# Gathering the last 8 rows of one tile in sixteen by a transfer of their own

## The chip, the cores and the metric

The kernel runs on one core of a Trainium2 chip. The metric is the device time of one execution in microseconds (us); the time quoted for a version is the median of its runs. A profile shows one execution, taken apart by engine: PE (matrix multiplications), DVE and ACT (elementwise work), POOL (here it issues the gathers), SP (here it issues loads and stores), and the 16 DMA engines that move the data.

## What is computed

```python
def setup_inputs():
    B, S, N, D = (16, 4096, 2048, 512)
    return {'x': np.random.randn(B, S, D).astype(np.float32), 'indices': np.sort(np.stack([np.random.choice(S, N, replace=False) for _ in range(B)]), axis=1).astype(np.int64), 'w': np.random.randn(D, D).astype(np.float32)}

def reference(x, indices, w):
    ...
    gathered = x[b_idx, indices, :].copy()
    cs = np.cumsum(gathered, axis=1)
    return np.matmul(cs, w).astype(np.float32)
```

From each of 16 batches 2048 of 4096 rows (512 fp32 numbers, 2 KB each) are picked by a sorted list of indices, summed cumulatively along the list, and multiplied by one 512x512 matrix. 67 MB are read and 67 MB are written.

## The kernel before

The list is cut into tiles of 128 rows (P): 16 tiles in a batch (NT), 256 in all (T). Two tiles make a group (R = 2, G = 128 groups). A tile goes through six steps, each on its own engine, and every engine has its own list of steps with waits on semaphores between them:

1. gather (`gather`, lines 129 to 145, POOL): one indirect DMA at line 139 brings 128 rows, one to a partition, into a slot of `g32`. There are 16 slots (NG), so tile t may be gathered once tile t-16 has been cast; that is the wait on `s_c` in line 132, taken for a whole group. Each slot has its own completion semaphore `s_g[t % 16]`. The row numbers of the first 4 tiles come from a small table `idx_first`, those of all others from `idxg`, which is prepared at the start.
2. cast (`cast`, line 154, ACT): fp32 to fp16, `g32` to `g16`, in the middle of the run two tiles at once. It waits for the gather.
3. sums (`sums`, line 166, PE): four 128x128x128 matmuls with a triangular matrix into PSUM `pa` give the running sums within the tile, transposed.
4. carry (`carry`, lines 185 and 198, DVE): adds the last column of the tile before and writes `cst` in fp16. Line 185 is the copy for the first tile of a batch, where nothing is carried in.
5. project (`project`, line 210, PE): four matmuls with the 512x512 weights into `pb`.
6. drain (`drain`, line 222, ACT) and store (line 245, SP): `pb` to `ob` in fp32, then one store of 1 MB for each two groups.

The order on each engine is written out by hand. ACT does, for u = 0 to 255, the casts listed in `casts[u]` (up to 6 tiles ahead of u) and then the drain of tile u (`step`, lines 393 to 401). PE runs the sums of a tile up to LEAD = 3 tiles or so ahead of the projections. POOL issues the 256 gathers one after the other (lines 308 and 309) and has little else to do after the start. DVE, PE and ACT run the middle of the work in a loop over 16 tiles; POOL and SP have all steps written out. Buffers: 16 slots of `g32`, 16 tiles of `g16`, 4 of `pa`, 8 of `cst`, 4 of `pb`, 16 tiles of `ob`.

At the start SP and ACT load the small index tables (line 251), SP the full index list (line 259), and both the weights, two quarters each (line 264); ACT casts quarters 0 and 1 (line 392), DVE quarters 2 and 3 (line 337), and PE waits for all four before the first projection.

Of the kernel before, what the change touches and what calls it, by code (L numbers as in the profile page):

```python
# [7 lines left out]
P = 128  # L8
FP32 = mybir.dt.float32
FP16 = mybir.dt.float16  # L10
U32 = mybir.dt.uint32
# [22 lines left out]
def kernel(  # L34
# [7 lines left out]
    nc = tc.nc  # L42

    B, S, D = x.shape
    N = indices.shape[1]
    R = 2
    Q = P // R
    DC = D // P
    NT = N // P
    T = B * NT  # L50
    G = T // R
    GB = NT // R
    KI = T // P
    FIRST = 2 * R
    NG = 16
    LEAD = 3
# [2 lines left out]
    NA = 4  # L59
    NB = 4  # L60
    NC = 4
    W = 2
    H = 1
    NO = 4
    U = NT
    V = max(U, W * R * NO)
    assert V % U == 0 and V % (W * R * NO) == 0 and T % V == 0 and U % NG == 0 and U % NA == 0 and U % (R * NC) == 0 and U % NB == 0
    assert D == 512 and N % (R * P) == 0 and T % P == 0

    x_flat = x.rearrange("b s d -> (b s) d")  # L70

    const = ctx.enter_context(tc.tile_pool(name="const", bufs=1))
    ps = ctx.enter_context(tc.tile_pool(name="ps", bufs=1, space=bass.MemoryType.PSUM))

    idx_first = const.tile([P, FIRST, 2], U32)
    idx64 = const.tile([P, KI, 2 * P], U32)
    idxf = const.tile([P, KI, P], FP32)
    idxg = const.tile([P, KI, P], U32)
    w32 = const.tile([P, DC, D], FP32)
# [6 lines left out]
    g32 = [const.tile([P, R, D], FP32, name=f"g32_{i}") for i in range(NG // R)]  # L86
# [8 lines left out]
    def sem(name):  # L95
        return tc.alloc_semaphore(name)
# [4 lines left out]
    s_first = [sem(f"s_first{k}") for k in range(2)]  # L101
    s_w = [sem(f"s_w{c}") for c in range(DC)]
    s_idx = [sem(f"s_idx{k}") for k in range(KI)]
    s_ol = sem("s_ol")
    s_g = [sem(f"s_g{i}") for i in range(NG)]
    s_o = [sem(f"s_o{i}") for i in range(NO)]
# [5 lines left out]
    pool, pe, dve, act, sp = (  # L112
        Lane(e) for e in (nc.gpsimd, nc.tensor, nc.vector, nc.scalar, nc.sync)
    )
# [14 lines left out]
    def gather(t):  # L129
        g, r = divmod(t, R)  # L130
        if t >= NG:
            pool.need(s_c, cast_by[R * (g + 1) - NG - 1])
        if t < FIRST:
            pool.need(s_first[g], 16)
            ap = idx_first[:, t, 0:1]
        else:
            pool.need(s_prep, t // P + 1)
            ap = idxg[:, t // P, t % P : t % P + 1]
        nc.gpsimd.indirect_dma_start(  # L139
            out=g32[g % (NG // R)][:, r, :],  # L140
            out_offset=None,
            in_=x_flat,
            in_offset=bass.IndirectOffsetOnAxis(ap=ap, axis=0),
            element_offset=(t // NT) * S * D,
        ).then_inc(s_g[t % NG], 16)

    PLAIN = (0, 1, G - 2, G - 1)
# [1 line left out]
    def cast(t, n, first=None):  # L150
        g, r = divmod(t, R)
        for u in range(t, t + n):
            act.need(s_g[u % NG], 16 * (u // NG + 1), first)
        nc.scalar.copy(  # L154
            out=g16[g % NH][:, r : r + n], in_=g32[g % (NG // R)][:, r : r + n]
        ).then_inc(s_c, 1)
# [91 lines left out]
    with nc.allow_non_contiguous_dma(reason="a few indices, one per partition"):  # L248
        for k, eng in enumerate((nc.sync, nc.scalar)):
            t = k * R  # L250
            eng.dma_start(
                out=idx_first[:, t : t + R, :],
                in_=indices[0, t * P : (t + R) * P]
                .bitcast(U32)
                .rearrange("(t p w) -> p t w", p=P, w=2),
            ).then_inc(s_first[k], 16)
    idx_rows = indices.bitcast(U32).rearrange("b (t q) -> (b t) q", q=2 * P)
    for k in range(KI):
        nc.sync.dma_start(
            out=idx64[:, k, :], in_=idx_rows[k * P : (k + 1) * P, :]  # L260
# [10 lines left out]
    for i in range(G // W - NO, G // W - 1):  # L271
# [8 lines left out]
        out=ident[:],  # L280
        in_=ident[:],
# [7 lines left out]
        out=ut[:],  # L289
        in_=ut[:],  # L290
# [9 lines left out]
        out=uq[:],  # L300
        in_=uq[:],
# [6 lines left out]
    for t in range(T):  # L308
        gather(t)
# [10 lines left out]
    nc.vector.memset(zeros[:], 0.0).then_inc(s_z, 1)  # L320
    for k in range(KI):
        dve.need(s_idx[k], 16)
        nc.vector.tensor_copy(out=idxf[:, k, :], in_=idx64[:, k, 0::2]).then_inc(s_if, 1)  # L323
    busy(9)
    for k in range(KI):
# [3 lines left out]
            out=pb[k % NB][:, :P], in_=idxf[:, k, :], identity=ident[:]  # L329
# [21 lines left out]
    done = 0  # L351
    for u in range(T):
        lead = 1 if min(u, T - 1 - u) < R * R else min(LEAD, 2 + (u + 4) // 16, 2 + (T - 1 - u) // 15)
        first = u if u // R in PLAIN else u // R * R + R - 1
# [38 lines left out]
    def step(u, first=None):  # L393
        if first is None and u == min(W * R * NO, 2 * U - 1):
            act.need(s_of, 16 * (R + W - 1 - H))
        if u % (W * R) == 0:
            stored = first if first is None else first * (16 * H) // (R * W * NO)
            act.need(s_o[u // R // W % NO], 16 * H * (u // R // W // NO), stored)
        for t, n in casts[u if first is None else 2 * U + u]:
            cast(t if first is None else t - 2 * U, n, first)  # L400
        drain(u, first)
# [40 lines left out]
```

## Time and profile before

| what | us |
|---|---|
| median of 3 runs (lowest, highest) | 438.41 (437.76, 445.43) |
| the profiled execution | 440.94 |
| its span, from the first to the last instruction | 439.2 |
| PE matmul busy | 329.8 |
| ACT busy | 263.6 |
| POOL busy | 243.7 |
| DVE busy | 178.4 |

How to read it: busy times are sums over instructions of one engine, so that an engine with less than 439.2 us has waited for the rest. The mean granted clock of PE was 0.892 of full speed. The page also gives the mean busy share of the 16 DMA engines in 40 slices of the span, and for each queue the packets that they moved; it doesn't tell the 16 engines apart. A row of an instruction group ends with the idle time of the engine just before these instructions and the releaser of most of it.

### The profile page before, as it was taken

The numbers are of one execution on the slowest core, as the hardware profiler recorded it, in microseconds if no ns is written. First come the engines' busy times: TensorE is split into PE (matmuls) and PEld (weight loads), VectorE is DVE, ScalarE is ACT, GpSimd is POOL, SyncE is SP. The second block draws the span as 40 slices with busy tenths as digits, with TensorE's granted clock in tenths as the row PEclk, the third lists the DMA queues.
The fourth block names the chain that finished last, engine by engine and source line by source line (L and its number), as shares of the span: only waits on it lengthen the run. The fifth ranks groups of instructions, "written<-read, shape, count | busy, mean of one in ns | idle before, by whom it ended". The sixth has DMA issues, their size and how long they took to land.

```text
span 439.2 us, 6408 instructions
## 1 busy us (share of the span) xinstructions
PE 329.8 (75%) x2066; PEld 171.5 (39%) x2066; DVE 178.4 (41%) x263; ACT 263.6 (60%) x407; POOL 243.7 (55%) x266
## 2 busy tenths in 40 slices
PE   6518687777877786679787697768777697876995
PEld 2203343343434343335344353434334343443552
DVE  2104343444344444345344344344345353543552
ACT  4216566556665665576656575566576666665794
POOL 6764557565655566556565465565555665655300
PEclk9756989798989899988899698996989969998898
DMA  7864979799888999989898899988989999999966
GB/s 225 256 212 156 347 273 344 252 336 364 285 318 304 333 351 328 350 294 339 316 353 295 310 336 335 359 318 273 366 310 328 331 337 328 300 330 349 331 242 241
DMA packets 39884, 135.68 MB, mean 309 GB/s; under 512 B 5825, under 2 KB 6081, under 8 KB 39873
## 3 DMA queue, kind: packets, MB, share of 16 engines
q0 software_dynamic: 20480, 67.13, 47.9%
q1 hardware_dynamic: 18832, 67.90, 38.9%
q10 hardware_dynamic: 560, 0.53, 0.4%
q8 instruction: 5, 0.08, 0.1%
q14 instruction: 7, 0.05, 0.0%
HBM read 68.42 MB, written 67.11 MB: 309 GB/s over the span
## 4 chain that ended last, share of the span: by engine, by line
PE 74%; issue 10%; DVE 7%; another core or an unknown queue 7%; ACT 1%; DVEq 0%; ACTq 0%; SPq 0%
PE pb L210 55%; PE pa L166 18%; DVE cst L198 7%; PE pb L316 1%; DVE cst L185 0%; ACT ob L222 0%; ACT g L154 0%; PE pb L328 0%; DVEq L26 0%; DVE zeros L320 0%; DVEq L437 0%; ACTq L26 0%; SPq L93 0%
## 5 line engine op out<-in xcount | busy, mean ns | idle before, releaser
L210 PE MATMUL pb<-w,cst 128*128 128x512 f16 x1024 | 293.1, 414 | 84.7 <-DVE cst L198 60.1
L139 POOL DMA_INDIRECT g<-in_x_dram,idxg x252 | 238.2, 945 | 165.1 <-ACT g L154 97.6
L198 DVE TENSOR_TENSOR cst<-pa,cst 128x512 f16<-128x512 f32 x240 | 166.1, 692 | 231.3 <-PE pa L166 162.2
L222 ACT COPY ob<-pb 128x512 f32<-128x512 f32 x256 | 146.2, 591 | 164.6 <-PE pb L210 108.1
L210 PEld LDWEIGHTS pb<-w,cst 128*128 128x128 f16 x1024 | 94.3, 104 | 164.9 <-DVE cst L198 65.8
L154 ACT CAST g<-g 128x1024 f16<-128x1024 f32 (+1 forms) x147 | 138.4, 945 | 0.3 <-issue 0.2
L166 PE MATMUL pa<-ut,g 128*128 128x128 f16 x992 | 103.9, 230 | 16.0 <-issue 12.8
L166 PEld LDWEIGHTS pa<-ut,g 128*128 128x128 f16 x992 | 81.5, 104 | 87.7 <-issue 33.8
L185 DVE CAST cst<-pa 128x512 f16<-128x512 f32 x16 | 11.0, 686 | 16.2 <-PE pa L166 12.6
L316 PE MATMUL pb<-zeros 128*128 128x512 f16 x16 | 5.9, 538 | 1.5 <-DVE zeros L320 1.5
L139 POOL DMA_INDIRECT g<-in_x_dram,idx_first x4 | 4.0, 994 | 1.6 <-issue 0.9
L166 PE MATMUL pa<-uq,g 128*128 128x128 f16 x32 | 3.1, 219 | 1.9 <-issue 1.8
L166 PEld LDWEIGHTS pa<-uq,g 128*128 128x128 f16 x32 | 2.2, 97 | 4.2 <-issue 3.1
L316 PEld LDWEIGHTS pb<-zeros 128*128 128x128 f16 x16 | 2.1, 135 | 4.2 <-issue 2.2
L392 ACT CAST w<-w 128x512 f16<-128x512 f32 x2 | 1.1, 616 | 3.4 <-DMA w<-in_w_dram 3.4
L389 ACT ACT_TABLE_LOAD x1 | 1.3, 1283 | 2.5 <-issue 2.5
L323 DVE CAST idxf<-idx 128x128 f32<-128x128 uint32 x2 | 0.5, 227 | 3.8 <-DMA idx<-in_indices_dram 3.8
L337 DVE CAST w<-w 128x512 f16<-128x512 f32 x2 | 0.8, 422 | 1.6 <-DMA w<-in_w_dram 1.6
L328 PE MATMUL pb<-ident,idxf 128*128 128x128 f32 x2 | 0.9, 447 | 0.0
L328 PEld LDWEIGHTS pb<-ident,idxf 128*128 128x128 f32 x2 | 0.4, 206 | 0.9 <-issue 0.9
L320 DVE MEMSET zeros<- 128x256 uint32 x1 | 0.3, 272 | 1.1 <-SPq L93 1.1
L334 DVE CAST idxg<-pb 128x128 uint32<-128x128 f32 x2 | 0.6, 292 | 0.3 <-PE pb L328 0.2
(11 smaller groups left out, 2.1 us busy)
## 6 DMA issues: line engine op xcount, KB each, us to landing
out_dram<-ob SPq DMA_DIRECT2D x62, 1024.0 KB
g<-in_x_dram,idxg POOLq DMA_INDIRECT x252
out_dram<-ob SPq DMA_DIRECT2D x4, 256.0 KB, 2.8
out_dram<-ob SPq DMA_DIRECT2D x2, 512.0 KB, 3.4
w<-in_w_dram ACTq DMA_DIRECT2D x2, 256.0 KB, 3.3
w<-in_w_dram SPq DMA_DIRECT2D x2, 256.0 KB
idx<-in_indices_dram SPq DMA_DIRECT2D x2, 128.0 KB, 2.6
g<-in_x_dram,idx_first POOLq DMA_INDIRECT x4
```

Of the source, the lines that this page charges most:

```text
L139: nc.gpsimd.indirect_dma_start(out=g32[g % (NG // R)][:, r, :], out_offset=None, in_=x_flat, in_offset=bass.IndirectOffsetOnAxis(ap=ap, ax ...
L154: nc.scalar.copy(out=g16[g % NH][:, r : r + n], in_=g32[g % (NG // R)][:, r : r + n]).then_inc(s_c, 1)
L166: mm = nc.tensor.matmul(out=pa[t % NA][:, c], lhsT=g16[g % NH][:, r, c * P : (c + 1) * P], rhs=uq[:] if first is None and g in PLAIN else ...
L185: nc.vector.tensor_copy(out=dst, in_=src).then_inc(s_d, 1)
L198: nc.vector.tensor_tensor(out=dst, in0=src, in1=last, op=mybir.AluOpType.add).then_inc(s_d, 1)
L210: mm = nc.tensor.matmul(out=pb[u % NB][:], lhsT=cst[g % NC][:, c, j, :], rhs=w16[:, c, :], start=(c == 0), stop=(c == DC - 1),)
L222: nc.scalar.copy(out=ob[g // W % NO][:, g % W, j], in_=pb[u % NB][:]).then_inc(s_e, 1)
L316: nc.tensor.matmul(out=pb[NB - 1][:], lhsT=zeros[:, :P], rhs=zeros[:], start=True, stop=True)
L328: nc.tensor.transpose(out=pb[k % NB][:, :P], in_=idxf[:, k, :], identity=ident[:]).then_inc(s_pt, 1)
L337: nc.vector.tensor_copy(out=w16[:, c, :], in_=w32[:, c, :]).then_inc(s_wc, 1)
L389: nc.scalar.copy(out=spare[:], in_=zeros[:, :1])
L392: nc.scalar.copy(out=w16[:, c, :], in_=w32[:, c, :]).then_inc(s_wc, 1)
```

## The change

In each batch the ninth tile (t % 16 == 8, SPLIT = NT // 2) is gathered by two transfers instead of one. First comes an instruction that puts the cursor of the software-generated transfers back to its start, then a transfer of the last 8 rows (E = 8) with row numbers from a new table `idx_last`, then one of the first 120 rows. The 8 rows report to a semaphore of their own, `s_h`, and the 120 rows to `s_g` as before. The cast of such a tile waits for both. `idx_last` (8 partitions, 16 batches) is loaded once at the start, by a DMA on ACT's queue between the small index table and the weights, and POOL waits for it once (`s_last`). The other 15 tiles of a batch are gathered as before. That makes 16 resets and 272 gathers in place of 256. Nothing on PE, DVE or SP changes, and on ACT only the waits and the one load.

```diff
+    E = 8
+    SPLIT = NT // 2
...
+    idx_last = const.tile([E, B, 2], U32)
...
-        nc.gpsimd.indirect_dma_start(
-            out=g32[g % (NG // R)][:, r, :],
-            out_offset=None,
-            in_=x_flat,
-            in_offset=bass.IndirectOffsetOnAxis(ap=ap, axis=0),
-            element_offset=(t // NT) * S * D,
-        ).then_inc(s_g[t % NG], 16)
+        parts = [(0, P, ap, s_g[t % NG])]
+        if t % NT == SPLIT:
+
+            pool.need(s_last, 16)
+            nc.gpsimd.inc_swdge_sem([], [], mode="reset_dge_cursor")
+            parts = [
+                (P - E, P, idx_last[:, t // NT, 0:1], s_h),
+                (0, P - E, ap[: P - E], s_g[t % NG]),
+            ]
+        for a, b, ap, done in parts:
+            nc.gpsimd.indirect_dma_start(
+                out=g32[g % (NG // R)][a:b, r, :],
+                out_offset=None,
+                in_=x_flat,
+                in_offset=bass.IndirectOffsetOnAxis(ap=ap, axis=0),
+                element_offset=(t // NT) * S * D,
+            ).then_inc(done, 16)
...
             act.need(s_g[u % NG], 16 * (u // NG + 1), first)
+            if u % NT == SPLIT:
+                act.need(s_h, 16 * (u // NT + 1), first)
...
+        nc.scalar.dma_start(
+            out=idx_last[:],
+            in_=indices[:, (SPLIT + 1) * P - E : (SPLIT + 1) * P]
+            .bitcast(U32)
+            .rearrange("b (p w) -> b p w", w=2)
...
+        ).then_inc(s_last, 16)
```

More of the change, by code (lines that the diff above doesn't have):

```diff
@@ L66 @@
     V = max(U, W * R * NO)
-    assert V % U == 0 and V % (W * R * NO) == 0 and T % V == 0 and U % NG == 0 and U % NA == 0 and U % (R * NC) == 0 and U % NB == 0
+    assert U == NT == NG and V % U == 0 and V % (W * R * NO) == 0 and T % V == 0 and U % NG == 0 and U % NA == 0 and U % (R * NC) == 0 and U % NB == 0
     assert D == 512 and N % (R * P) == 0 and T % P == 0
@@ L103 @@
     s_idx = [sem(f"s_idx{k}") for k in range(KI)]
+    s_last = sem("s_last")
+    s_h = sem("s_h")
     s_ol = sem("s_ol")
@@ L256 @@
             ).then_inc(s_first[k], 16)
+        nc.scalar.dma_start(
+            out=idx_last[:],
+            in_=indices[:, (SPLIT + 1) * P - E : (SPLIT + 1) * P]
+            .bitcast(U32)
+            .rearrange("b (p w) -> p b w", w=2),
+        ).then_inc(s_last, 16)
     idx_rows = indices.bitcast(U32).rearrange("b (t q) -> (b t) q", q=2 * P)
```

## The prediction

> **What bounds the kernel now.** I read the page first, then the waits, then busy time by stretch, then the timeline of one stretch in the middle. From the list of instruction groups:
>
> ```profile
> L210 PE MATMUL pb<-w,cst 128*128 128x512 f16 x1024 | 293.1, 414 | 84.7 <-DVE cst L198 60.1
> L139 POOL DMA_INDIRECT g<-in_x_dram,idxg x252 | 238.2, 945 | 165.1 <-ACT g L154 97.6
> L222 ACT COPY ob<-pb 128x512 f32<-128x512 f32 x256 | 146.2, 591 | 164.6 <-PE pb L210 108.1
> L154 ACT CAST g<-g 128x1024 f16<-128x1024 f32 (+1 forms) x147 | 138.4, 945 | 0.3 <-issue 0.2
> ```
>
> The last row decides. The cast is the only reader of gathered rows, and in 147 casts ACT was idle 0.3 us before one: in this execution no cast waited for a gather. The second row says the reverse: it is POOL that waits, 97.6 us, for casts to free slots. So gathers run as far ahead as 16 slots allow. Counting along POOL's and ACT's lists, the gather of tile 116 is issued at 188.19 us and its cast begins at 212.41, 24 us later.
>
> The list of waits, longest first in total (us, times, longest):
>
> ```profile
> DVE cst L198 <- PE pa L166: 162.2, 118, 5.7
> ACT ob L222 <- PE pb L210: 108.1, 81, 3.5
> POOL g L139 <- ACT g L154: 97.6, 42, 5.1
> ```
>
> DVE and ACT wait for PE. PE's full pace shows in the starts of its projections, 205.81, 206.90, 207.98: 1.087 us a tile, 256 tiles x 1.087 = 278 us, and at the granted clock of 0.892 312 us. The span is 439.2, so 127 us are neither. The timeline says what some of that is (start, us, engine, and in brackets the idle time before and its releaser):
>
> ```profile
> 206.67 0.39 PE L166 MATMUL pa<-ut,g 128*128 128x128 f16 x4
> ...
> 209.48 0.95 POOL L139 DMA_INDIRECT g<-in_x_dram,idxg  x1 [0.30 <-issue]
> ...
> 211.87 0.69 DVE L185 CAST cst<-pa 128x512 f16<-128x512 f32 x1 [4.29 <-PE pa L166]
> ...
> 213.41 1.04 PE L210 MATMUL pb<-w,cst 128*128 128x512 f16 x4 [2.71 <-DVE cst L198]
> 213.72 0.94 POOL L139 DMA_INDIRECT g<-in_x_dram,idxg  x1 [3.29 <-ACT g L154]
> ```
>
> The sums at 206.67 are those of tile 112; their reader, the carry at L185, starts 4.8 us after the matmuls are recorded as done (207.06). PE's word comes late; then DVE, ACT, PE and POOL stand still in turn. By stretch (busy us and number for PE, PEld, DVE, ACT, POOL; PE clock; DMA share; GB/s):
>
> ```profile
> 204.00:208.00 4.00, 4.00 (x33) 2.28 (x31) 1.91 (x3) 3.16 (x5) 3.02 (x4) 1.00 1.04 362
> 208.00:212.00 4.00, 2.49 (x19) 1.16 (x16) 0.13 (x1) 0.66 (x2) 1.89 (x2) 1.00 0.98 363
> 212.00:216.00 4.00, 2.59 (x12) 1.18 (x13) 3.33 (x5) 3.86 (x6) 1.89 (x2) 0.83 0.69 214
> ```
>
> The DMA engines are full while PE's word is late (0.98) and slack when work resumes (0.69). So the DMA engines are no idle bystander: between 50 and 400 us their share is 0.87 to 0.94. Why PE is late I can't tell; that it goes with full DMA engines I see. The change touches them in two ways.
>
> **What the Trainium skill says.** "DMA: Bandwidth & Descriptors", section "Why a DMA increments its semaphore by 16 and not by 1": a transfer runs on the largest number up to 16 that divides its slowest dimension; with fewer than 16, the software path takes consecutive engines from a round-robin cursor, and all 16 report completion whatever the shape. So 8 rows go to 8 engines and 120 rows to 15. If the reset sets the cursor to 0 (the page has no reset), these are 0 to 7, then 8 to 15 and 0 to 6, and engine 7 is left out. Same page, "Latency and other measured facts": engines 7 and 15 are usually slower, cause uncertain. That is the gain to be had; this page of the profile doesn't separate the engines, so no row agrees or disagrees. What agrees is the packet count: 20480 on the gather queue is 80 a gather, 16 completions and 64 of two rows.
>
> **The change, part by part.**
>
> Engine loads. In 16 tiles an engine gathers 16 x 8 = 128 rows; after, engine 7 has 121, engines 0 to 6 129, engines 8 to 15 128. Gathers are 67.13 of 135.68 MB, so engine 7 loses 7/128 x 0.495 = 2.7% of its bytes and seven engines gain 0.4%. If engine 7 sets the pace throughout, that is 0.027 x 439.2 = 11.9 us; if nobody waits for it, 0. As no cast waits for a gather, I take 0. Stores (no row shows a wait for one in mid-run: "DMA out" releases 2.2 us, at the end) don't raise it.
>
> POOL. 16 more gathers. A 128-row gather takes 0.945 us and 0.30 of issue; the 8-row one costs between the issue alone and the full 1.25. I take 1.25, as the part that rows cost is unknown. The 120-row one I take as unchanged, up to 1.25 more if its shape is slow. The reset isn't in this trace: between 0 and the 0.30 of a step, taken at 0.1. Per batch 1.35 us (0.3 to 2.8), 16 x 1.35 = 22 us of POOL. The cover is POOL's 97.6 us of waiting for casts, 6.1 a batch, and behind it the 24 us between issue and cast: the split tile and those behind it land some 1.35 us later and still wait. Cost 0. Were the cover gone, it would be the full 22 us. POOL has nothing else queued behind these but gathers; SP's stores aren't passed by it.
>
> ACT. One more wait in 16 casts, on a semaphore raised long before: below the 0.3 us that all 147 casts wait now. Queued behind is the drain of the same step, which holds `pb`, which holds PE; as the wait is met, 0.
>
> Completions and packets. Per batch 16 more completions and 8 one-row packets in place of 4 two-row ones: 20 more packets in 1280, some 320 in all, of completion or half size. Below 0.5% of DMA work, or 2 us if the DMA engines set the end; taken at 0.
>
> Start. The new load stands ahead of ACT's two weight loads and delays them by one issue, 0.49 us (the first index load on that queue). They land 3.3 us after issue at 1.5 and 2.1, near 5.4, then 5.9; ACT's cast of the weights starts at 7.44, when quarter 0 from SP's queue, issued at 2.49, has come. Cover 1.5 us; cost 0, and 0.5 if it is gone. POOL's wait for the table falls before the ninth gather, at 13.40, long after. Nothing more is stored or multiplied.
>
> Sum against the profiled execution: 439.2 + 0 in the span, 440.94 + 0 in all, which stands 2.5 above the median of 438.41. On the median: 438.41 + 0, rounded to 438.5.
>
> **Rivals.**
>
> Relief: engine 7 is the straggler that the full DMA stretches wait for, and PE's word comes when it is done. For it: DMA share near 1 while PE is late. Against it: no cast waits for a gather, and engine 15 stays as it was. Time: at most 438.4 - 11.9 = 426.5; likelier half, as the next engine takes over, 432.5.
>
> Longer bursts, the slower side: POOL issues in bursts (203.24 to 210.43, then a wait to 213.72), and PE's late word ends near the end of such a burst. If late signals last as long as gathers are being written, each batch's extra 1.35 us stretches one burst and the standstill with it: 16 x 1.35 = 22 us, 460; half of it, if only bursts near the limit count, 449. It decides from some 0.55 us a batch (8.8 us, 2%). For it: the coincidence above. Against it: the cause may run the other way, as standing ACT ends POOL's burst.
>
> The change doesn't do what it says: the reset doesn't place the cursor at 0, or 120 rows go to fewer engines. At another cursor the relief falls on another engine: 438.5 again. With 8 engines for 120 rows each gets 15 in place of 8 once in 16 tiles, 7/128 more rows on each such engine, 2.7% more bytes: up to 450.
>
> **How the numbers follow.** Hidden altogether: 0.66, range 434 to 443 (packets and start above, a little relief below). Relief: 0.15, half of it over 2%. Longer bursts: 0.14, nearly all over 2%. Misplaced: 0.05, half each way. A time below 429.6 is faster by over 2%, one above 447.2 slower, which is about what a measurement of this kernel can tell from no change (three runs lie between 437.76 and 445.43). Faster: half of the relief and a little, 0.09. Slower: 0.13 of bursts, 0.02 misplaced, 0.01, together 0.16. Same: 0.75. The range takes in half the relief and the half price of the bursts: 431 to 449.
>
> **What would show it.** Right: the 120- and 8-row gathers appear as 32 rows of POOL near 0.95 us or less; POOL's wait for casts falls from 97.6 by about 22; the cast's idle time stays below 1 us; 20800 packets on the gather queue; DVE's wait for PE stays near 162. Relief would show as DVE's and ACT's waits for PE falling by some 10 us. Longer bursts would show as those waits growing. Wrong altogether: the cast waiting for gathers, or a reset that takes microseconds.

## The result, and the profile after

| | median, us (lowest to highest, runs) |
|---|---|
| before | 440.81 (437.76 to 445.43, 4) |
| after | 465.93 (461.47 to 467.15, 4) |
| ratio, with its 95% interval | 1.058 [1.045, 1.070] |

The change costs 25 us, 5.8%. The forecast was 438.5, within 431 to 449. The profiled execution took 465.24 us with a span of 463.3, 24.1 more than the span of 439.2 before. Ratios are taken over comparable runs only, so they can differ a little from the quotient of the medians given. Every comparison is with runs of the kernel before on the same chip, which matters here: that kernel takes 436 to 448 us on the chips of the first runs and 349 to 352 us on those of the last ones, for a reason that no run shows.

The groups of instructions of the kernel after, to be set beside the four rows shown of before:

```profile
L227 PE MATMUL pb<-w,cst 128*128 128x512 f16 x1024 | 297.4, 418 | 103.4 <-DVE cst L215 86.3
L154 POOL DMA_INDIRECT g<-in_x_dram,idxg x252 | 240.5, 954 | 140.1 <-ACT g L171 70.7
...
L171 ACT CAST g<-g 128x1024 f16<-128x1024 f32 (+1 forms) x147 | 138.3, 944 | 0.3 <-issue 0.2
...
L154 POOL DMA_INDIRECT g<-in_x_dram,idx_last x16 | 14.4, 900 | 32.5 <-ACT g L171 27.9
```

Casts still wait for nothing (0.3 us), so the gathers are not late. A gather of 8 rows takes POOL 0.900 us, nearly as long as one of 128 (0.945 before). PE's projections now wait 86.3 us for DVE in place of 60.1. PE's matmuls themselves take 335.3 us in place of 329.8 (the granted clock is 0.877 in place of 0.892), so slower matmuls are at most 5.5 us of the 24; the rest is waiting.

The longest waits of the kernel after (us in total, times, longest):

```profile
DVE cst L215 <- PE pa L183: 172.1, 115, 4.3
POOL g L154 <- ACT g L171: 98.6, 43, 5.0
...
ACT ob L239 <- PE pb L227: 91.8, 73, 4.8
PE pb L227 <- DVE cst L215: 86.3, 38, 7.6
POOL g L154 <- issue: 75.0, 228, 1.9
```

DVE's wait for PE grew by 9.9 us. A further wait of DVE, whose releaser the profile can't place (it writes `remote`), grew by 23.1 us; first before, then after:

```profile
DVE cst L198 <- remote: 44.7, 16, 12.6
```

```profile
DVE cst L215 <- remote: 67.8, 21, 11.2
```

POOL does 16.7 us more (260.4 busy in place of 243.7), and its idle time before gathers has not shrunk to make room: 98.6 us for casts (97.6 before) and 75.0 between issues (68.4 before). Busy time and these two waits come to 409.7 before and 434.0 after. The difference, 24.3, is the growth of the span (24.1) to within 0.2. It isn't lost at the start or the end: the stretch from 50 to 250 us, first before and then after (busy us and number for PE, PEld, DVE, ACT, POOL; PE clock; DMA share; GB/s):

```profile
50.00:250.00 200.00, 151.67 (x963) 79.25 (x962) 84.36 (x123) 122.62 (x186) 116.25 (x123) 0.91 0.90 319
```

```profile
50.00:250.00 200.00, 147.44 (x917) 77.10 (x918) 79.41 (x116) 117.21 (x179) 117.49 (x124) 0.88 0.85 302
```

POOL issues as many gathers in 200 us as before (124 against 123), but of these some 7 are now of 8 rows. Data moves at 302 GB/s in place of 319, and PE, DVE and ACT get through some 4 to 6% fewer instructions in the stretch. POOL's timeline around one split tile of the kernel after:

```profile
204.64 0.90 POOL L154 DMA_INDIRECT g<-in_x_dram,idx_last  x1 [1.60 <-ACT g L171]
205.84 1.00 POOL L154 DMA_INDIRECT g<-in_x_dram,idxg  x1 [0.30 <-issue]
207.15 0.99 POOL L154 DMA_INDIRECT g<-in_x_dram,idxg  x1 [0.31 <-issue]
208.44 0.96 POOL L154 DMA_INDIRECT g<-in_x_dram,idxg  x1 [0.31 <-issue]
...
216.44 0.95 POOL L154 DMA_INDIRECT g<-in_x_dram,idxg  x1 [3.28 <-ACT g L171]
```

0.90 and 0.30 for the transfer of 8 rows, and 0.05 + 0.04 + 0.01 for neighbours that take a little longer than 0.95: about 1.3 us more, as forecast. The reset is no row of its own and leaves no gap. The wait of 3.28 us that ends the burst stands as it did before (3.29).

### The profile page after: what moved, and what is told of

Its sections match the earlier page's. It is cut to its first block, busy times and chain, and to the rows that moved or that the text cites. A ratio compares the mean times of both kernels' runs of the same rounds, so it can differ in the third digit from the quotient of the medians.

```text
span 463.3 us, 6444 instructions
## 1 busy us (share of the span) xinstructions
PE 335.3 (72%) x2066; PEld 174.1 (38%) x2066; DVE 178.7 (39%) x263; ACT 264.1 (57%) x407; POOL 260.4 (56%) x282
## 4 chain that ended last, share of the span: by engine, by line
PE 68%; another core or an unknown queue 13%; DVE 9%; issue 6%; DMA 1%; SPq 0%; ACT 0%; DVEq 0%
PE pb L227 51%; PE pa L183 18%; DVE cst L215 9%; DMA w<-in_w_dram 1%; ACT ob L239 0%; DVE w L360 0%; SPq L282 0%; DVE cst L202 0%; DVEq L26 0%; ACT g L171 0%; SPq L268 0%; SPq L287 0%; SPq L460 0%; SPq L96 0%
## 5 line engine op out<-in xcount | busy, mean ns | idle before, releaser
L227 PE MATMUL pb<-w,cst 128*128 128x512 f16 x1024 | 297.4, 418 | 103.4 <-DVE cst L215 86.3
L227 PEld LDWEIGHTS pb<-w,cst 128*128 128x128 f16 x1024 | 95.6, 106 | 187.0 <-DVE cst L215 93.4
L183 PE MATMUL pa<-ut,g 128*128 128x128 f16 x992 | 105.7, 233 | 14.6 <-issue 14.3
L183 PEld LDWEIGHTS pa<-ut,g 128*128 128x128 f16 x992 | 82.5, 105 | 86.0 <-issue 33.7
L154 POOL DMA_INDIRECT g<-in_x_dram,idx_last x16 | 14.4, 900 | 32.5 <-ACT g L171 27.9
```

Source lines behind the costliest of these rows:

```text
L154: nc.gpsimd.indirect_dma_start(out=g32[g % (NG // R)][a:b, r, :], out_offset=None, in_=x_flat, in_offset=bass.IndirectOffsetOnAxis(ap=ap, ...
L183: mm = nc.tensor.matmul(out=pa[t % NA][:, c], lhsT=g16[g % NH][:, r, c * P : (c + 1) * P], rhs=uq[:] if first is None and g in PLAIN else ...
L227: mm = nc.tensor.matmul(out=pb[u % NB][:], lhsT=cst[g % NC][:, c, j, :], rhs=w16[:, c, :], start=(c == 0), stop=(c == DC - 1),)
```

## The experiments

Accounts of the missing 24 us that had to be told apart, with their numbers in the texts put on record before each run: POOL's extra time (theory 1); the reset (2), or which DMA engines the two parts fall on and in what shapes (3); the wait that the cast has for a second semaphore; more work for the DMA engines; or the added gather itself, as a transfer that POOL's software makes, while it is under way (4).

### What part of the change it is (first kind of chip)

Kernel before, with the reset alone:

```diff
+        if t % NT == NT // 2:
+            nc.gpsimd.inc_swdge_sem([], [], mode="reset_dge_cursor")
```

> The kernel before, with the cursor reset ahead of the ninth gather of each batch and nothing else: no split, no new table. Theory 1 (any extra time of POOL in a burst of gathers is added to the end): the reset is short, so within 3 us of the 440.8 of before. Theory 2 (the reset itself disturbs the queue of gathers, by some 1.5 us each time): 16 x 1.5 = 24 us more, near 465. Theory 3 (the uneven shapes of 8 and 120 rows on the DMA engines cost the time): no change.

446.7 us (437.62 to 452.37, 20 runs) beside 444.9; ratio 0.991 [0.984, 0.999], which rests on only two of the 20. The medians differ by 1.8 us, in a spread of 15. By neither number is the reset more than a small part of the 25 us.

Kernel after, without the reset:

```diff
-            nc.gpsimd.inc_swdge_sem([], [], mode="reset_dge_cursor")
```

> The changed kernel without the reset: the 8 and the 120 rows go to whichever engines come next. Theory 1: near 464, since POOL still issues 16 more gathers. Theory 2: back near 441. Theory 3: near 464, too, as the shapes stay; if it matters which engine is left out, some us away from 465.9.

467.35 us (466.86 to 474.78, 4); 1.046 [1.039, 1.054]. The change had 1.058 [1.045, 1.070]; the intervals overlap, and most of the cost, if not all, stays. So it doesn't hang on where the cursor stands.

Kernel after, without the reset and cut into 64 and 64 rows:

```diff
-    E = 8
+    E = 64
...
-            nc.gpsimd.inc_swdge_sem([], [], mode="reset_dge_cursor")
```

> The split at 64 and 64 rows, without the reset: as many gathers on POOL as in the changed kernel, but both transfers divide evenly over the 16 DMA engines, 4 rows each. The new table at the start is 64 instead of 8 rows deep, 1024 small packets in place of 128, for which I allow 1 us. Theory 1: near 465. Theory 2: near 441. Theory 3: near 441.

471.69 us (469.07 to 476.76, 4); 1.060 [1.051, 1.069]. In its profile the first drain starts at 18.88 us where it is 12.08 in the run without reset, so some 7 us of it are lost once, at the start; the rest is the cost of the split again. Two even parts are no cheaper than an uneven pair: neither 8 rows nor 120 is a bad shape.

### POOL's time, DMA work, or a gather (first kind of chip)

Each of these three is the kernel before, with one thing added per batch. First, POOL busy with a memset of some 0.96 us:

```diff
+        if t % NT == NT // 2:
+            pool.need(s_idle, t // NT)
+            nc.gpsimd.memset(idle[:], 0.0).then_inc(s_idle, 1)
```

> The kernel before, with one memset of 128x1024 fp32 on POOL ahead of the ninth gather of each batch: some 1 to 1.5 us of POOL's time and no DMA work. The resets alone cost nothing, the split at 8 and 120 rows without reset and the split at 64 and 64 cost as much as the change, so the cost comes with the second gather. Theory 1 (POOL's own time is on the path): 16 x 1 to 1.5 us more than before, 457 to 469. Theory 4 (it is the second gather as a piece of DMA work, with its own descriptors and completions, not POOL's time): within 4 us of before, near 441 to 448.

445.52 us (440.51 to 452.35, 20) beside 442.65; 1.0045 [1.001, 1.008], 2 us. Second, a gather of 8 rows into a spare buffer that nobody reads:

```diff
+        if t % NT == NT // 2:
+            pool.need(s_x, 16 * (t // NT))
+            nc.gpsimd.indirect_dma_start(
+                out=extra[:8],
...
+                in_offset=bass.IndirectOffsetOnAxis(ap=ap[:8], axis=0),
...
+            ).then_inc(s_x, 16)
```

> The kernel before, with a gather of 8 rows into a spare tile ahead of the ninth gather of each batch. Nothing waits for it but its own successor a batch later; the ninth gather keeps its 128 rows, and no table is loaded. Theories 1 and 4: as the change, 463 to 470, since POOL issues as many gathers. If instead the later arrival of the split tile, or the wait on two semaphores, costs the time: within 4 us of before.

468.1 us (466.4 to 469.1, 4); 1.060 [1.051, 1.069]: 26.6 us, 1.66 for each of the 16. Two runs that give POOL almost the same time side by side; POOL's groups and its waits, first with the memset,

```profile
L143 POOL MEMSET idle<- 128x1024 f32 x16 | 15.3, 955 | 28.1 <-ACT g L159 27.0
```

```profile
POOL g L144 <- ACT g L159: 55.9, 27, 4.3
POOL idle L143 <- ACT g L159: 27.0, 10, 3.8
```

and then with the gather of 8 rows:

```profile
L143 POOL DMA_INDIRECT extra<-in_x_dram,idxg x16 | 14.1, 884 | 23.8 <-ACT g L165 20.8
```

```profile
POOL g L150 <- ACT g L165: 79.3, 38, 3.9
...
POOL extra L143 <- ACT g L165: 20.8, 6, 7.3
```

With the memset POOL's waits for casts fall from 97.6 to 55.9 + 27.0 = 82.9, by 14.7, which is what the 15.3 us of memsets took: cover, as the prediction had it. With the gather they are 79.3 + 20.8 = 100.1. POOL had 14.1 us more to do, and waited no less. (The 97.6 are of the profile before, of an earlier run; the next run below, on the chip of these two, has 103.8.) So on these chips POOL's time is covered and a gather is not, though no one waits for its data. The second semaphore of the cast isn't needed for the cost either. The price of 1.66 us is close to the kernel's own pace: before, POOL issued 123 gathers in 200 us, one each 1.63 us. A gather of 8 rows, then, adds about as much time as one of 128 rows takes up on average; no run on this kind of chip added one of 128.

Third, DMA work without POOL: one more load of 128 rows (256 KB) on SP's queue in each batch, 4.2 MB in all, 3% of the traffic.

```diff
+        if g % GB == 2 * W:
+            sp.need(s_x, 16 * b)
+            nc.sync.dma_start(out=extra[:], in_=x_flat[b * S : b * S + P, :]).then_inc(s_x, 16)
```

> The kernel before, with one more load of 128 rows of 2 KB per batch from SP's queue into a spare tile that nobody reads: 4 MB of DMA work more (3%), 16 more completions a batch, nothing on POOL. Theory 1: within 4 us of before. If DMA work of any kind is on the path: 256 KB take some 0.65 us at the 400 GB/s of full stretches, so 16 x 0.65 = 10 us more, near 455.

442.5 us (438.61 to 446.45, 20) beside 442.65; 1.002 [0.998, 1.005]. Sixteen times the rows of the added gathers, moved from SP's queue in 144 packets each where a gather of 8 rows makes 32, cost nothing that shows. It is not the load on the DMA engines, in bytes or in packets.

Last, no gather at all: SP loads every second row of each tile's half in its place, as many bytes, in the order in which the steps need them. POOL is left with 1.5 us of work.

```diff
-        nc.gpsimd.indirect_dma_start(
+        nc.sync.dma_start(
+            out=g32[g % (NG // R)][:, r, :], in_=x_even[b, h * P : (h + 1) * P, 0, :]
         ).then_inc(s_g[t % NG], 16)
```

> The gathers are left out: each tile is loaded by an ordinary DMA from SP's queue, 128 rows of 2 KB, every second row of x, in place of the rows that the indices name; as many bytes to the same slots, and POOL has nothing to do after the start. Theory 1: well below before, since POOL's 20 us of issue a batch are gone: PE's 312 us plus start and end, 340 to 400. If the DMA work is the bound and not who issues it: near 440.

349.7 us (349.67 to 349.84, 4); 0.792 [0.785, 0.798]. Its waits, and its stretch from 100 to 300 us (columns as above):

```profile
DVE cst L190 <- PE pa L158: 145.6, 237, 1.9
ACT g L146 <- DMA out_dram<-ob: 69.8, 53, 2.2
```

```profile
100.00:300.00 200.00, 170.65 (x1210) 89.70 (x1209) 104.43 (x152) 148.51 (x228) 0.00 (x0) 1.00 1.03 403
```

The DMA engines are full throughout (1.03), moving 403 GB/s, and yet DVE never waits longer than 1.9 us for PE, where before it was 5.7. So full DMA engines alone are not what delays PE's word. PE's granted clock is 0.99 in these four runs, where the kernel before has 0.89 to 0.93 on the same chip: the lower clock isn't fixed by the chip. In this run the gathers are gone, and with them the standstills, 93 us worth.

### The same on the other kind of chip

The runs that follow fell on chips where the kernel before takes 350 us. Both kernels once more, unchanged:

> The kernel before, for its profile on the same chip. Where it takes 350 us, casts should wait for gathers and stores (DMA), POOL hardly for casts, and the DMA engines should be busy to 0.95 or more; where it takes 440 us, the profile should look like the first one: casts wait for nothing, POOL for casts.

350.04 us (348.85 to 351.34, 16) beside 350.01; 1.000 [0.999, 1.001].

> The changed kernel as it is, on whichever chip comes. Where before takes some 440 us: 465 again. Where before takes some 350 us: if the DMA engines are the bound there and the left-out engine is the slowest one, up to 2.7% less, 341 to 348; if an added gather costs what it cost in the runs with 64 of them (75/64 = 1.2 us), 16 x 1.2 = 19 us more, 369; if only its DMA work counts, 350 to 352.

362.99 us (362.63 to 363.26, 5); 1.037 [1.035, 1.038]: 13.0 us, half of what it costs on the other chips. Waits of the kernel before there, then of the kernel after:

```profile
DVE cst L198 <- PE pa L166: 139.2, 236, 1.9
...
POOL g L139 <- issue: 71.0, 233, 0.3
ACT g L154 <- DMA g<-in_x_dram,idxg: 69.8, 92, 1.9
...
POOL g L139 <- ACT g L154: 6.7, 22, 0.3
```

```profile
ACT g L171 <- DMA g<-in_x_dram,idxg: 86.8, 75, 4.1
...
POOL g L154 <- ACT g L171: 4.0, 13, 0.3
```

By its profile it is another kernel. POOL hardly waits for casts (6.7 us): it issues one gather after the other, and the casts wait for gathers (69.8, then 86.8). POOL has no waiting left that could cover anything. The gathers' own view gives the sum. First and last start are in it, before and then after, and the page gives the spans of 347.1 and 361.3:

```profile
L139 POOL DMA_INDIRECT g<-in_x_dram,idxg x252: 942/946/955, 8.4 to 322.1; - x126
...
DMA to landing us min/median/max: 3.6/9.0/13.8
```

```profile
L154 POOL DMA_INDIRECT g<-in_x_dram,idxg x252: 942/946/1124, 8.4 to 343.2; - x126
```

The last gather starts 21.1 us later, 16 x 1.32, which is the forecast's price of a batch (1.35). From there to the end it was 25.0 us and is 18.1. So 21.1 - 6.9 = 14.2 us remain in the span. Before, gathers land 9.0 us after issue, up to 13.8; after, the median is 6.6 and the longest 8.7. The DMA engines were behind POOL, and 7 us of this backlog are all the cover there is.

If that is so, the memset must cost as well here. The kernel with the memset again:

> The kernel before with one memset of 0.955 us on POOL ahead of the ninth gather of each batch, no DMA work. Where before takes 350 us and POOL's time is the path: 16 x 0.95 to 1.25 us less what POOL can still hide (some 6 us): 359 to 366. If the change's cost there is DMA work: 350 to 352. Where before takes 440 us: no change, as measured.

356.09 us (355.71 to 356.52, 4) beside 349.86; 1.018 [1.014, 1.022]. In its gathers' view (span 354.0),

```profile
L144 POOL DMA_INDIRECT g<-in_x_dram,idxg x252: 942/946/998, 8.4 to 335.5; - x126
...
DMA to landing us min/median/max: 3.5/6.8/8.5
```

the last gather starts 13.4 us later than before, and the tail is 18.5 us, the backlog gone (8.5 at most): 13.4 - 6.5 = 6.9, and 6.2 measured. POOL's time alone explains the loss on these chips; on the others the memset cost 2 us.

Three sizes of the added transfer, one to a batch or one to four tiles; what was expected of them reckons with the 442 us of the first kind of chip, on which they did not fall. A gather of all 128 rows that nobody reads:

```diff
-                out=extra[:8],
+                out=extra[:],
...
-                in_offset=bass.IndirectOffsetOnAxis(ap=ap[:8], axis=0),
+                in_offset=bass.IndirectOffsetOnAxis(ap=ap, axis=0),
```

> As the extra gather once a batch, but of 128 rows in place of 8, 4 MB more in all. Theory 4 with a price a gather: 468, as with 8 rows; with a price a row: 442 + 16/256 of the 90 us between the kernels with and without gathers is 448, and the 8 rows would have cost next to nothing, which they did not; with both: up to 468 + 10 for the DMA work.

362.99 us (362.58 to 363.19, 4) beside 349.84; 1.037 [1.034, 1.039]. That is the time of the change itself on another chip of this kind. Rows cost nothing here, gathers do. Next, 64 gathers of 8 rows:

```diff
-        if t % NT == NT // 2:
-            pool.need(s_x, 16 * (t // NT))
+        if t % 4 == 0:
+            pool.need(s_x, 16 * (t // 4))
```

> As the extra gather of 8 rows into a spare tile, but ahead of every fourth gather: 64 extra ones in place of 16. Theory 4 (each gather through the software path costs the whole kernel some 1.6 us, however few rows it moves, and POOL's time is not the reason): 442 + 64 x 1.6 = 545. Theory 6 (the first extra gather of a batch only upsets a rhythm of 16, the rest find cover): 465 to 490.

424.41 us (423.09 to 429.59, 4); 1.217 [1.209, 1.225]: 74.6 us, 1.17 each. Its last gather starts at 403.7, 81.6 later than before, and again 7 are given back. Then a plain transfer of 8 rows in place of the gather, also made by POOL's software:

```diff
+            nc.gpsimd.dma_start(
+                out=extra[:8], in_=x_flat[t * P : t * P + 8, :]
+            ).then_inc(s_x, 16)
```

> As the extra gather of 8 rows, once a batch, but an ordinary DMA of 8 neighbouring rows issued on POOL's queue, with no indices. Theory 4a (any software transfer costs it): near 468. Theory 4b (the indirect form costs it): 441 to 446.

353.56 us (353.23 to 354.26, 4); 1.010 [1.007, 1.013]. It takes POOL 0.560 us, and its last gather starts at 331.9, 9.8 later, of which 3.7 are left in the median.

### Is there a gain behind the cost?

To see a relief of one engine, POOL needs room. Kernel before, with one tile in four loaded by SP from fixed rows, as in the run without gathers, and the other 192 gathered:

```diff
     for t in range(T):
-        gather(t)
+        if t % 4 != 3:
+            gather(t)
```

> Every fourth tile is loaded by SP (every second row of x, not the rows that the indices name), the other three are gathered: 192 software gathers in place of 256, as many bytes. Theory 4: 64 x 1.6 = 102 us less, but not below the 349.7 of the kernel with no gathers: 350 to 365. If a gather's cost is not a fixed price that adds up, but the mere mixture of gathers and stores slows the DMA engines: a quarter of the way from 442 to 350, near 419.

346.46 us (345.72 to 346.69, 4); 0.989 [0.986, 0.992]. This was meant for the first kind of chip, to see whether fewer gathers mean fewer standstills. Once more, on another chip:

> Every fourth tile loaded by SP (every second row of x, not the rows that the indices name), 192 software gathers in place of 256. Where before takes 350 us: 346, as measured. Where it takes 440 us: 440 - 64 x 1.6 = 338 if the price goes with the number of gathers, bounded by the DMA engines to 350 to 360; near 418 if it doesn't.

346.65 us (346.45 to 346.86, 2) beside 350.01; 0.990 [0.988, 0.992]. This chip was of the second kind again, so that question stays open. What both show is that POOL now waits 101.6 and 103.3 us for casts, and the time falls by only 1%: there the DMA engines are the bound: ACT waits 69.0 us for stores ahead of its casts. This is the place where a straggler among them would show. The same kernel with the whole split, and the same without the reset, so that the parts go to whichever engines come next:

> The kernel with every fourth tile loaded by SP (every second row of x, not the rows that the indices name) and 192 gathers, 346.6 us where before takes 350, with the whole change on top: reset, 8 rows, 120 rows. POOL waits 102 us for casts there and can hide 16 x 1.3 us. If the engine that is left out is the slowest and sets the pace: down by up to 2.7%, 337 to 344. If all engines are alike: 346 to 350. If the split costs DMA time of its own: above 350.

349.52 us (348.86 to 351.77, 20) beside 349.86; 0.999 [0.998, 1.001].

> The same without the reset, so that the engine left out moves on from batch to batch. If the relief of one certain engine is what counts: 346 to 350, and slower than with the reset by some 3 to 9 us. If all engines are alike: the same as with the reset, within 1 us.

349.51 us (347.68 to 351.62, 20); 0.999 [0.997, 1.001]. POOL's wait for casts, without the split, with it, and with it but no reset:

```profile
POOL g L139 <- ACT g L165: 101.6, 102, 2.3
```

```profile
POOL g L154 <- ACT g L182: 69.3, 52, 2.7
```

```profile
POOL g L153 <- ACT g L181: 78.7, 76, 2.5
```

With POOL waiting 69 to 79 us, the split still costs 3 us (349.5 against 346.5 on other chips of this kind), with the reset and without it. No relief shows, and no cost of the reset either. Where the 3 us come from stays open. No version that gathers all rows was clearly faster than the kernel before.

## Why the prediction was wrong, step by step

**The step that failed** is "Cost 0", with its ground, "The cover is POOL's 97.6 us of waiting for casts, 6.1 a batch, and behind it the 24 us between issue and cast". The price beside it, 16 x 1.35 = 22 us of POOL, was right in size: 1.3 us a batch in the timeline, 21.1 us in all on the chips where nothing else disturbs. "Were the cover gone, it would be the full 22 us" gives 460 from the same sum; it was 465.93, and the other 6 us are not accounted for.

Why the cover was none, the runs show in part. POOL's waiting is spare for a memset (14.7 of 15.3 us absorbed) and not for a gather (100.1 us of waiting with 16 gathers more, 97.6 without). So the wait is no reserve that stands apart from the gathers: where an added gather goes in, the waiting behind it stays as long. Taking out all gathers took 93 us and the long waits for PE with them, on the same chip; on the second kind of chip the same gathers leave no wait for PE over 1.9 us. Together this says that on the first kind of chip the standstills come with gathers, and that one more gather adds to the time beside them. That a gather under way holds up PE's word of completion fits all of it, but is only argued: no view shows what PE's word waits for.

**"The DMA engines are full while PE's word is late"** was read as a sign that they are part of the cause. The run without gathers has them full all the time, and PE prompt. Nor is a share near 1 a sign that no more could be moved: on the second kind of chip, between 50 and 300 us, the run with 64 added gathers has a share of 0.95 at 338 GB/s and the kernel before 1.03 at 413.

**Longer bursts**, the rival at 0.14, had the side and nearly the size (460). Its ground, "late signals last as long as gathers are being written", is what the runs support; its measure, POOL's extra 1.35 us, is not, as the memset takes POOL 15.3 us, the added gathers 14.1, and the memset costs 2 us. The objection put against it, that standing ACT ends POOL's burst and the cause runs the other way, weighed too much.

**Relief** has nothing for it. The time rose, and it made no difference whether the reset was to fix the engine left out (346.5 without the split, 349.5 with the reset and 349.5 without it). The Trainium skill ("DMA: Bandwidth & Descriptors", section "Latency and other measured facts") has engines 7 and 15 as usually slower; nothing here shows it, and no view shows which engine was left out.

**Packets.** 20800 were expected on the gather queue, and the page after has

```profile
q0 software_dynamic: 20992, 67.13, 45.3%
```

so 32 more a batch and not 20. The sizes of all packets tell where the other 12 are; before, after, and with the added gather of 8 rows alone:

```profile
DMA packets 39884, 135.68 MB, mean 309 GB/s; under 512 B 5825, under 2 KB 6081, under 8 KB 39873
```

```profile
DMA packets 40531, 135.69 MB, mean 293 GB/s; under 512 B 6408, under 2 KB 6664, under 8 KB 40520
```

```profile
DMA packets 40395, 135.95 MB, mean 293 GB/s; under 512 B 6208, under 2 KB 6464, under 8 KB 40384
```

Packets between 2 and 8 KB, the third figure less the second, are 33792, 33856 and 33920. So an added gather of 8 rows makes 8 of them, one a row, and 24 under 512 B, where the prediction had only the 16 completions that the Trainium skill states for each transfer ("DMA: Bandwidth & Descriptors", section "Why a DMA increments its semaphore by 16 and not by 1"). In the change these large packets grow by 64, 4 a batch: 8 for the 8 rows and 60 for the 120 rows, in place of 64. Of the 32 more a batch, the 8 rows account for all, so the 120 rows make 80 like any gather of 128: 60 of two rows and 20 small ones. Sixty is what the prediction's 15 engines with four each would carry, so an engine does seem to be left out. The 12 small packets too many, 8 and 4, are as many as the engines left out would have carried of large ones; that is a reading which fits, as no row names an engine. The time doesn't hang on it, as the run without reset and the run with halves show.

**Right** were: no cast waits for a gather (0.3 us); the cast's second semaphore isn't needed for the cost; the reset costs little or nothing; POOL's rows are near 0.95. The start, taken at 0 with 0.5 as its upper end, may be a little more, or this is spread: the first drain comes at 13.05 us in place of 11.87, but at 12.08 in the run without reset, which has the same load.

**Open**: why PE's word is late on one kind of chip and not on the other, where the same kernel takes 350 us. The queue rows give one trace of it: gather packets took 47.9% of 439.2 us on the first kind, 210 us, and 50.0% of 347.1 on the second, 174 us, while those of SP's queue, nearly all stores, took 171 and 169; whether that is cause or effect no run tells. Open too: whether the sizes of the added transfer, measured on the second kind, hold on the first, and whether fewer gathers, or a plain transfer by POOL's software in place of a gather, shorten the standstills there.

## What to carry to other kernels

The idle time of an engine may come from the very work that it issues; then it covers other work and not more of the same. Here it covered a memset and not a gather. Before a step is costed at nothing on it, add work of the same kind there, and then work of another kind, and compare. A gather costs POOL about 1.2 us whether it brings 8 rows or 128, so cutting one in two doubles its price; do that only if a run has shown that a DMA engine is late.

## What the hardware showed unasked

- One kernel, two kinds of chip: 436 to 448 us on some and 349 to 352 us on others, with the granted PE clock at 0.892 and 0.993 in the profiles. On a chip of the slower kind the kernel without gathers takes 349.7, at a clock of 0.992.
- A gather takes POOL 0.946 us for 128 rows and 0.88 to 0.90 for 8, with 0.30 to the next; a plain transfer by POOL's software 0.560 for 8 rows.
- An added gather of 8 rows costs 1.66 us on one kind of chip and, at 64 of them, 1.17 on the other; a memset of 0.955 us costs 0.1 us on the first and, at 0.969, 0.4 on the second.
- A gather of 8 rows makes 32 packets, 24 of them under 512 B; one of 120 rows 80, 20 of them small; one of 128 rows 80, 16 of them small.
- On one core, 413 GB/s were moved from 50 to 300 us (kernel before, second kind of chip).
